# The last branch of a hybrid decoder layer: merge and weight splits in a fixed order on ScalarE, VectorE and POOL

## The chip, the cores and the metric

The kernel runs on one core of a Trainium2 chip. The metric is the time of one execution on the device in microseconds (us). Before the change it is 1801.29 us, the median of three runs (1801.08 to 1802.17). All times below that name a place in the program are counted from the start of the profiled execution's span.

## The reference

One decoder layer on 1024 tokens of width 1024, all in float32. Three branches (an RWKV-7 recurrence, a stick-breaking attention and a cross-attention into 256 memory tokens) each give 512 columns per token. They are projected, gated, summed and projected again; a convolutional feed-forward network follows.

```python
h = rms_norm(x, norm1_g[l])
proj = h @ w_in[l]
p_rwkv, p_sb, q_mem, gate_logits = jnp.split(proj, cut, axis=-1)
y_a, v_first = rwkv7_branch(p_rwkv, ...)
y_b = stick_breaking_branch(p_sb, ...)
y_m = memory_branch(q_mem, mem, ...)
ys = jnp.stack([y_a, y_b, y_m], axis=2)
branch_out = jnp.einsum('btnc,ncd->btnd', ys, w_branch[l])
gates = jax.nn.sigmoid(gate_logits.reshape(b, t, N_BRANCH, D_MODEL))
merged = jnp.sum(gates * branch_out, axis=2)
x = x + merged @ w_out[l]
x = x + conv_ffn(x, norm2_g[l], w_up[l], conv_w[l], conv_b[l], w_down[l])
```

The place in question is `branch_out` and `merged` for the first branch (`y_a`, done last, because its recurrence ends last), and the start of `merged @ w_out`.

## The kernel before

**Products in three parts.** Each float32 operand is split into a high part, rounded to the format that TensorE multiplies fast, and a low part, the remainder. A product is the sum of three: high by high, high by low, low by high (`mm3`). So every weight tile of 128 x 1024 that comes from HBM is split before use (`split_raw`): ScalarE copies it into the high part (line 80), POOL subtracts that from the raw tile and writes the low part (line 81). Raw tiles arrive through `load_w` on SP's queue, in two buffers named `wr`. A new load into such a buffer can only be issued after POOL's half of the split that read it.

**The last branch** (`branch_last`). `y` holds the first branch's output, split, in four tiles. The result is made in eight blocks d = 0 to 7 of 128 output columns each, over all 1024 tokens in two halves. For a block, TensorE runs 24 matmuls (four tiles of `y`, three parts, two halves) into one pair of PSUM banks. Four banks named `mm` make two pairs, which the blocks use in turn. A branch weight `w_br` serves two blocks, so there are four of them. Then:

- VectorE multiplies each half in PSUM by the gate tile `g`, loaded from `gsd` (line 1286). This frees the bank.
- VectorE adds the partial sum `o` of the other two branches, loaded from `mrd` (line 1287).
- ScalarE copies the result into the high part of the merged tile `mg` (line 1293: one piece of 512 tokens, two of 256), VectorE subtracts and writes the low part (line 1294).

**The output projection** (`out_proj`) follows. It takes the merged tiles as stationary operand and eight tiles of `w_out`, split by `load_wo`, as moving one. The first four of these splits are called for inside `branch_last`, at d = 2 to 5, the other four in `out_proj`. Its first step computes two token tiles at once, in both pairs of banks, with 12 matmuls for each of the eight weight tiles.

**What sets the order.** Most of the program leaves the order of instructions on an engine to a scheduler, which works with estimated times. `keep_in_program_order` fixes an instruction's place among the others that are marked so, on its engine. In `branch_last` nothing is marked. Buffers limit the loads: there are seven `at` tiles, four of which hold `y`, so three are left for the gates, and a fourth gate waits until block 0's last subtraction; three `w4` tiles hold the partial sums. SP issues its DMAs in one order, and a DMA whose buffer is not free holds back those behind it.

In front of the last branch stands the last gate block: TensorE makes the logits, ScalarE empties the banks (line 820), VectorE multiplies (line 821), ScalarE applies the sigmoid (line 824) and stores (line 826). Block 1 of the last branch uses the banks that line 820 empties. Line 1192 is VectorE's half of the split of `y`.

Of the kernel before, what the change touches and what calls it, by code (L numbers as in the profile page):

```python
# [11 lines left out]
F32 = mybir.dt.float32  # L12
F32R = mybir.dt.float32r
BF16 = mybir.dt.bfloat16
AF = mybir.ActivationFunctionType
ALU = mybir.AluOpType
# [33 lines left out]
class Trunk:  # L50
# [25 lines left out]
        self.nc.sync.dma_start(raw, src)  # L76
        return raw

    def split_raw(self, raw, hi, lo):
        self.nc.scalar.activation(hi, raw, AF.Copy)  # L80
        self.nc.gpsimd.tensor_tensor(lo, raw, hi.bitcast(F32), ALU.subtract)  # L81
        return hi, lo

    def split_w(self, src):
        raw = self.load_w(src)
        hi = self.pool_wt.tile([128, 1024], F32R, name=self.nm("wh"), tag="wh", bufs=2)
        lo = self.pool_wt.tile([128, 1024], F32R, name=self.nm("wl"), tag="wl", bufs=2)
        return self.split_raw(raw, hi, lo)

    def mm3(self, outs, w, x, first, last):  # L90
        for pi, (a, b) in enumerate(((0, 0), (0, 1), (1, 0))):
# [1159 lines left out]
            items.append(self.branch_item(b, d, st, first))  # L1251
        return load, hooks, items

    def load_wo(self, k):
        slots = ["qk"] * 8 + ["at"] * 6 + ["it", "sp"]
        hl = [self.pool_l.tile([128, 1024], F32R, name="wo_sp", tag="sp", bufs=1) if s == "sp" else self.t4(s, F32R) for s in slots[2 * k : 2 * k + 2]]
        self.wo.append(self.split_raw(self.load_w(self.I["w_out"][k]), *hl))

    def branch_last(self):
        nc = self.nc  # L1260
        self.wo = []
        y = self.split_y(self.yT, True)
        mg = lambda name, shape: self.pool_l.tile(shape, F32R, name=name, tag="l4")
        self.mg0 = [[mg(f"mg0_{i}_{k}", [128, 2, 512]) for k in range(4)] for i in range(2)]
        self.mg1 = [[[mg(f"mg1_{i}_{t}_{k}", [128, 4, 256]) for k in range(2)] for t in range(2)] for i in range(2)]
        for d in range(8):
            if d % 2 == 0:
                w = self.split_w(self.I["w_br"][0, d // 2])
            g, o = self.t4("at"), self.t4()
            nc.sync.dma_start(g, self.gsd[0, d])  # L1270
            nc.sync.dma_start(o, self.mrd[d])
            pp = [self.ps("mm"), self.ps("mm")]
            if d == 0:
                for i, (a, b) in enumerate(((0, 0), (1, 0), (0, 1))):
                    for k in range(4):
                        for h in range(2):
                            self.mmul(pp[h], w[a][:, k * 256 : k * 256 + 128], y[k][b][:, h * 512 : (h + 1) * 512],
                                      start=(i == 0 and k == 0), stop=(i == 2 and k == 3))
            else:
                for k in range(4):  # L1280
                    self.branch_mm(d, w, y, pp, k)
            if d in (2, 3, 4, 5):
                self.load_wo(d - 2)
            for h in range(2):
                hs = slice(h * 512, (h + 1) * 512)
                nc.vector.tensor_tensor(g[:, hs], pp[h], g[:, hs], ALU.mult)
                nc.vector.tensor_tensor(g[:, hs], g[:, hs], o[:, hs], ALU.add)  # L1287
                if h == 0:
                    parts = [[self.mg0[i][d // 2][:, d % 2] for i in range(2)] + [slice(0, 512)]]
                else:  # L1290
                    parts = [[self.mg1[i][t][d // 4][:, d % 4] for i in range(2)] + [slice(512 + 256 * t, 768 + 256 * t)] for t in range(2)]
                for hi, lo, ts in parts:
                    nc.scalar.activation(hi, g[:, ts], AF.Copy)
                    nc.vector.tensor_tensor(lo, g[:, ts], hi.bitcast(F32), ALU.subtract)  # L1294

    def out_proj(self):
        nc = self.nc
# [745 lines left out]
```

## Time and profile before

| | |
|---|---|
| median of three runs | 1801.29 us |
| the profiled execution | 1802.26 us |
| its span, first to last instruction | 1800.5 us |
| mean granted TensorE clock | 0.999 |

The profile names engines as follows: PE is TensorE, PEld its weight loads, DVE VectorE, ACT ScalarE, POOL GpSimd; SPq is the queue of SyncE, which issues most DMAs. A row of the timeline gives start, length, engine, line, operation, the tile written and the tiles read, the count of instructions merged in it, and in brackets the engine's idle time ahead of the first of them and what ended it. A row of the waits names who waited for whom, with the total in us, the times and the longest. A row of the windows gives the stretch, its length, the busy time of the engine asked for with its count of instructions, the granted clock, the mean busy share of the DMA engines and what they moved in GB/s.

### The profile page before, as it was taken

What the parts mean: (1) busy time and instruction counts of PE and PEld (TensorE: products, weight loads), DVE (VectorE), ACT (ScalarE), POOL (GpSimd) and SP (SyncE); (2) the same over time, 40 slices, a digit from 0 to 9 for tenths busy, and PEclk for the clock granted to TensorE, in tenths of its full rate; (3) what the DMA queues carried; (4) which work ended last, traced back from release to release, by engine and by line L of the source; (5) the groups of instructions that cost most, each with busy time, mean ns of one, the idle gap of its engine ahead of it and who ended that gap; (6) DMA issues with size and microseconds to landing.
All of it is one profiled execution on the core that took longest, in us unless ns stands there. A gap on an engine that the chain in (4) does not pass through costs nothing.

```text
span 1800.5 us, 27327 instructions
## 1 busy us (share of the span) xinstructions
PE 1778.4 (99%) x10479; PEld 1443.3 (80%) x10479; DVE 1183.7 (66%) x1626; ACT 864.3 (48%) x1556; POOL 791.5 (44%) x448
## 2 busy tenths in 40 slices
PE   9999999999999999999999999999999999999999
PEld 6777778888888888777777878877888888888887
DVE  5667774898987625244443882587776777785496
ACT  6444344556566636544444334554544444454343
POOL 3223353322322462122423541587767767545454
PEclk9999999999999999999999999999999999999999
DMA  5155564211112352567654462322322323486475
GB/s 209 59 164 176 194 210 158 74 42 45 53 57 77 118 138 69 185 238 274 230 189 176 164 222 94 117 88 99 117 96 88 122 95 111 135 303 229 147 237 207
DMA packets 122773, 261.29 MB, mean 145 GB/s; under 512 B 28682, under 2 KB 43658, under 8 KB 122515
## 3 DMA queue, kind: packets, MB, share of 16 engines
q1 hardware_dynamic: 85026, 193.83, 32.5%
q10 hardware_dynamic: 33840, 53.10, 8.0%
q0 software_dynamic: 3776, 12.62, 2.3%
q8 instruction: 82, 1.34, 0.3%
q14 instruction: 49, 0.39, 0.1%
HBM read 178.99 MB, written 80.48 MB: 144 GB/s over the span
## 4 chain that ended last, share of the span: by engine, by line
PE 69%; DVE 6%; ACT 2%; issue 2%; POOL 2%; DMA 1%; SPq 0%; DVEq 0%; POOLq 0%; ACTq 0%
PE mm L115 57%; PE g L115 10%; PE g L105 3%; DMA wr<-in_w_out_dram 1%; DVE at L926 1%; DVE mg L1294 1%; DVE it L545 1%; DMA A<-yd 1%; DVE at L1287 0%; POOL wl L81 0%; POOL wl L1465 0%; DVE inst L547 0%; DVE gall L1550 0%; ACT at L1143 0%; DVE w L821 0%
## 5 line engine op out<-in xcount | busy, mean ns | idle before, releaser
L81 POOL TENSOR_TENSOR wl<-wr,wh 128x1024 fp32r<-128x1024 f32 (+2 forms) x78 | 195.9, 2513 | 501.9 <-ACT wh L80 492.2
L115 PE MATMUL mm<-xhi,wh 128*128 128x512 f32 x784 | 259.9, 412 | 0.5 <-DVE w L322 0.4
L115 PE MATMUL mm<-xlo,wh 128*128 128x512 f32 x784 | 243.7, 392 | 0.2 <-DVE xlo L199 0.2
L115 PE MATMUL mm<-xhi,wl 128*128 128x512 f32 x784 | 242.5, 391 | 0.0
L115 PEld LDWEIGHTS mm<-xlo,wh 128*128 128x128 f32 x784 | 147.2, 188 | 33.7 <-DVE xlo L199 0.9
L115 PEld LDWEIGHTS mm<-xhi,wl 128*128 128x128 f32 x784 | 146.9, 188 | 33.0 <-POOL wl L81 0.7
L115 PEld LDWEIGHTS mm<-xhi,wh 128*128 128x128 f32 x784 | 136.7, 189 | 28.9 <-issue 6.1
L80 ACT ACTIVATE wh<-wr 128x1024 fp32r<-128x1024 f32 (+2 forms) x78 | 81.8, 1048 | 146.2 <-PE mm L115 94.1
L115 PE MATMUL mm<-dw,da 128*128 128x512 f32 x528 | 120.3, 389 | 0.0
L115 PE MATMUL mm<-BT,l 128*128 128x512 f32 x504 | 117.9, 389 | 1.4 <-POOL l L1465 1.4
L115 PEld LDWEIGHTS mm<-dw,da 128*128 128x128 f32 x528 | 99.1, 188 | 20.6
L1754 POOL TENSOR_TENSOR dw<-draw,dw 128x512 fp32r<-128x512 f32 x55 | 82.0, 1498 | 76.4 <-ACT dw L1752 69.0
L115 PEld LDWEIGHTS mm<-BT,l 128*128 128x128 f32 x504 | 94.5, 188 | 21.4 <-POOL l L1465 1.8
L926 DVE TENSOR_TENSOR_SCAN at<-at,nrt 128x128 f32<-128x128 f32 (+3 forms) x64 | 94.2, 1478 | 25.5 <-ACT at L920 25.3
L115 PE MATMUL mm<-BT,wh 128*128 128x512 f32 x352 | 108.6, 389 | 0.9 <-DVE BT L1375 0.9
L115 PE MATMUL mm<-B,wh 128*128 128x512 f32 x352 | 108.4, 389 | 0.0
L1753 DVE TENSOR_TENSOR da<-draw,da 128x512 fp32r<-128x512 f32 x77 | 63.4, 830 | 50.9 <-ACT da L1751 50.7
L115 PE MATMUL g<-dw,da 128*128 128x512 f32 x396 | 90.2, 389 | 0.0
L1465 POOL TENSOR_TENSOR l<-it,l 128x1024 fp32r<-128x1024 f32 x21 | 50.8, 2419 | 88.9 <-ACT l L1462 88.8
L821 DVE TENSOR_TENSOR w<-w,nrt 128x1024 f32<-128x1024 f32 x24 | 49.8, 2076 | 58.5 <-ACT w L820 47.5
L115 PEld LDWEIGHTS g<-dw,da 128*128 128x128 f32 x396 | 74.3, 188 | 15.4
L1751 ACT ACTIVATE da<-draw 128x512 fp32r<-128x512 f32 x77 | 48.1, 628 | 79.2 <-PE mm L115 31.8
(335 smaller groups left out, 3990.0 us busy)
## 6 DMA issues: line engine op xcount, KB each, us to landing
wr<-in_w_in_dram SPq DMA_DIRECT2D x48, 512.0 KB, 3.6
draw<-actd SPq DMA_DIRECT2D x77, 256.0 KB, 3.2
draw<-in_w_down_dram SPq DMA_DIRECT2D x55, 256.0 KB, 4.5
at<-scr SPq DMA_DIRECT2D x24, 512.0 KB, 5.9
wr<-in_w_up_dram SPq DMA_DIRECT2D x22, 512.0 KB, 3.5
actd<-gall ACTq DMA_DIRECT2D x44, 256.0 KB, 3.2
rw<-in_w_up_dram SPq DMA_DIRECT2D x20, 512.0 KB, 3.6
gsd<-w ACTq DMA_DIRECT2D x18, 512.0 KB, 2.8
```

Of the source, the lines that this page charges most:

```text
L80: self.nc.scalar.activation(hi, raw, AF.Copy)
L81: self.nc.gpsimd.tensor_tensor(lo, raw, hi.bitcast(F32), ALU.subtract)
L105: self.pinned(self.nc.tensor.transpose(out, in_, self.ident[:n, :n]))
L115: self.pinned(self.nc.tensor.matmul(*a, **k))
L545: self.pinned(nc.vector.tensor_tensor(tv, X[:, 0:s, s : s + 1].to_broadcast([128, s, n]), X[:, s : s + 1, s + 1 : 64].to_broadcast([128, s ...
L821: nc.vector.tensor_tensor(g, g, self.nrb, ALU.mult)
L926: self.pinned(nc.vector.tensor_tensor_scan(sn[:, :W][:, ::-1], sn[:, :W][:, ::-1], self.nrt[:, 1152 - W :][:, ::-1], 1.0, ALU.mult, ALU.max))
L1294: nc.vector.tensor_tensor(lo, g[:, ts], hi.bitcast(F32), ALU.subtract)
L1465: ins = nc.gpsimd.tensor_tensor(lo, src, hi.bitcast(F32), ALU.subtract)
L1751: self.pinned(nc.scalar.activation(A[:, 0], a, AF.Copy))
L1753: self.pinned(nc.vector.tensor_tensor(A[:, 1], a, A[:, 0].bitcast(F32), ALU.subtract))
L1754: nc.gpsimd.tensor_tensor(Wt[:, 1], w, Wt[:, 0].bitcast(F32), ALU.subtract)
```

## The change

`split_raw`, `split_w` and `load_wo` get a parameter through which the caller can fix their instructions' order. `branch_last` uses it. The first two branch weights and the first output weight are called for ahead of the block loop; inside the loop each of blocks 0 to 4 calls for one more weight after its own work: output weight 1 after block 0, branch weight 2 after block 1, output weight 2 after block 2, branch weight 3 after block 3, output weight 3 after block 4. The multiplies, adds, copies and subtractions are marked as fixed, in the order two multiplies, two adds with the copies, three subtractions.

```diff
-    def split_raw(self, raw, hi, lo):
-        self.nc.scalar.activation(hi, raw, AF.Copy)
-        self.nc.gpsimd.tensor_tensor(lo, raw, hi.bitcast(F32), ALU.subtract)
+    def split_raw(self, raw, hi, lo, fix=lambda ins: ins):
+        fix(self.nc.scalar.activation(hi, raw, AF.Copy))
+        fix(self.nc.gpsimd.tensor_tensor(lo, raw, hi.bitcast(F32), ALU.subtract))
         return hi, lo
...
     def branch_last(self):
...
+        fix = self.tc.keep_in_program_order
+        ws = [self.split_w(self.I["w_br"][0, j]) for j in range(2)]
+        self.load_wo(0)
         for d in range(8):
-            if d % 2 == 0:
-                w = self.split_w(self.I["w_br"][0, d // 2])
+            w = ws[d // 2]
             g, o = self.t4("at"), self.t4()
...
-            if d in (2, 3, 4, 5):
-                self.load_wo(d - 2)
+            halves = []
             for h in range(2):
                 hs = slice(h * 512, (h + 1) * 512)
-                nc.vector.tensor_tensor(g[:, hs], pp[h], g[:, hs], ALU.mult)
-                nc.vector.tensor_tensor(g[:, hs], g[:, hs], o[:, hs], ALU.add)
+                fix(nc.vector.tensor_tensor(g[:, hs], pp[h], g[:, hs], ALU.mult))
+            for h in range(2):
+                hs = slice(h * 512, (h + 1) * 512)
+                fix(nc.vector.tensor_tensor(g[:, hs], g[:, hs], o[:, hs], ALU.add))
...
                 for hi, lo, ts in parts:
-                    nc.scalar.activation(hi, g[:, ts], AF.Copy)
-                    nc.vector.tensor_tensor(lo, g[:, ts], hi.bitcast(F32), ALU.subtract)
+                    fix(nc.scalar.activation(hi, g[:, ts], AF.Copy))
+                    halves.append((lo, g[:, ts], hi.bitcast(F32)))
+            for lo, x, hi in halves:
+                fix(nc.vector.tensor_tensor(lo, x, hi, ALU.subtract))
+            if d in (1, 3):
+                ws.append(self.split_w(self.I["w_br"][0, d // 2 + 2], fix))
+            elif d in (0, 2, 4):
+                self.load_wo({0: 1, 2: 2, 4: 3}[d], fix)
```

The built programs hold the same instructions, and TensorE and VectorE run them in the same order as before. On the three other engines the order differs, in the last branch alone.

ScalarE, from the split of the first output weight (`qk<-wr`) into block 1; `wh` are high parts of branch weights, L820 empties the gate block's banks, `mg` are the merged tiles. Before:

```order
L80 ACTIVATE qk_9574<-wr_9576 128x1024
L820 ACTIVATE w_1457_9410<-mm_9360 128x512
L820 ACTIVATE w_1457_9410<-mm_9361 128x512
L80 ACTIVATE wh_9540<-wr_9538 128x1024
L824 ACTIVATE w_1457_9410<-w_1457_9410 128x1024
L826 DMA gsd<-w_1457_9410 128x1024
L80 ACTIVATE qk_9620<-wr_9622 128x1024
L1293 ACTIVATE mg_0_0_9436<-at_9458 128x512
L1293 ACTIVATE mg_0_0_0_9444<-at_9458 128x256
L1293 ACTIVATE mg_0_1_0_9446<-at_9458 128x256
L80 ACTIVATE wh_9638<-wr_9636 128x1024
L1293 ACTIVATE mg_0_0_9436<-at_9498 128x512
```

ScalarE at the same place now (L1296 is the former L1293):

```order
L80 ACTIVATE qk_9464<-wr_9466 128x1024
L80 ACTIVATE wh_9460<-wr_9458 128x1024
L820 ACTIVATE w_1457_9410<-mm_9360 128x512
L820 ACTIVATE w_1457_9410<-mm_9361 128x512
L824 ACTIVATE w_1457_9410<-w_1457_9410 128x1024
L826 DMA gsd<-w_1457_9410 128x1024
L1296 ACTIVATE mg_0_0_9436<-at_9470 128x512
L1296 ACTIVATE mg_0_0_0_9444<-at_9470 128x256
L1296 ACTIVATE mg_0_1_0_9446<-at_9470 128x256
L80 ACTIVATE qk_9510<-wr_9512 128x1024
L1296 ACTIVATE mg_0_0_9436<-at_9516 128x512
```

The second output weight's split stood ahead of block 0's copies and stands behind them now; the second branch weight's split stood behind L820 and stands ahead of it.

POOL, the low parts of the splits of the last branch; `qk` and `at` belong to output weights, `wl` to branch weights. Before:

```order
L81 TENSOR_TENSOR qk_9575<-wr_9576,qk_9574 128x1024
L81 TENSOR_TENSOR wl_9541<-wr_9538,wh_9540 128x1024
L81 TENSOR_TENSOR qk_9621<-wr_9622,qk_9620 128x1024
L81 TENSOR_TENSOR wl_9639<-wr_9636,wh_9638 128x1024
L81 TENSOR_TENSOR qk_9673<-wr_9674,qk_9672 128x1024
L81 TENSOR_TENSOR qk_9719<-wr_9720,qk_9718 128x1024
L81 TENSOR_TENSOR wl_9737<-wr_9734,wh_9736 128x1024
L81 TENSOR_TENSOR at_9821<-wr_9822,at_9820 128x1024
```

POOL at the same place now:

```order
L81 TENSOR_TENSOR qk_9465<-wr_9466,qk_9464 128x1024
L81 TENSOR_TENSOR wl_9461<-wr_9458,wh_9460 128x1024
L81 TENSOR_TENSOR qk_9511<-wr_9512,qk_9510 128x1024
L81 TENSOR_TENSOR wl_9559<-wr_9556,wh_9558 128x1024
L81 TENSOR_TENSOR qk_9603<-wr_9604,qk_9602 128x1024
L81 TENSOR_TENSOR wl_9651<-wr_9648,wh_9650 128x1024
L81 TENSOR_TENSOR qk_9695<-wr_9696,qk_9694 128x1024
L81 TENSOR_TENSOR at_9821<-wr_9822,at_9820 128x1024
```

Output and branch weights alternate now; before, the third and fourth output weight followed each other ahead of the last branch weight.

SP's DMAs, from the second branch weight on; `at<-gsd` are gates, `w<-mrd` partial sums. Before:

```order
L76 DMA wr_9538<-in_w_br_dram 128x1024
L1270 DMA at_9458<-gsd 128x1024
L1270 DMA at_9498<-gsd 128x1024
L1270 DMA at_9544<-gsd 128x1024
L76 DMA wr_9576<-in_w_out_dram 128x1024
L1271 DMA w_1470_9459<-mrd 128x1024
L1271 DMA w_1474_9499<-mrd 128x1024
L76 DMA wr_9622<-in_w_out_dram 128x1024
L76 DMA wr_9636<-in_w_br_dram 128x1024
```

SP at the same place now (L1272 and L1273 are the former L1270 and L1271):

```order
L76 DMA wr_9458<-in_w_br_dram 128x1024
L1272 DMA at_9470<-gsd 128x1024
L76 DMA wr_9466<-in_w_out_dram 128x1024
L1272 DMA at_9516<-gsd 128x1024
L1272 DMA at_9562<-gsd 128x1024
L76 DMA wr_9512<-in_w_out_dram 128x1024
L1273 DMA w_1476_9471<-mrd 128x1024
L1273 DMA w_1483_9517<-mrd 128x1024
L76 DMA wr_9556<-in_w_br_dram 128x1024
```

The first output weight moved ahead of the gates of blocks 1 and 2, and the second one ahead of the partial sums of blocks 0 and 1.

More of the change, by code (lines that the diff above doesn't have):

```diff
@@ L77, in load_w, with split_w @@
         return raw
-    def split_raw(self, raw, hi, lo):
-        self.nc.scalar.activation(hi, raw, AF.Copy)
-        self.nc.gpsimd.tensor_tensor(lo, raw, hi.bitcast(F32), ALU.subtract)
+    def split_raw(self, raw, hi, lo, fix=lambda ins: ins):
+        fix(self.nc.scalar.activation(hi, raw, AF.Copy))
+        fix(self.nc.gpsimd.tensor_tensor(lo, raw, hi.bitcast(F32), ALU.subtract))
         return hi, lo
-    def split_w(self, src):
+    def split_w(self, src, fix=lambda ins: ins):
         raw = self.load_w(src)
@@ L87, in split_w @@
         lo = self.pool_wt.tile([128, 1024], F32R, name=self.nm("wl"), tag="wl", bufs=2)
-        return self.split_raw(raw, hi, lo)
+        return self.split_raw(raw, hi, lo, fix)
     def mm3(self, outs, w, x, first, last):
@@ L1252, in branch, with load_wo @@
         return load, hooks, items
-    def load_wo(self, k):
+    def load_wo(self, k, fix=lambda ins: ins):
         slots = ["qk"] * 8 + ["at"] * 6 + ["it", "sp"]
         hl = [self.pool_l.tile([128, 1024], F32R, name="wo_sp", tag="sp", bufs=1) if s == "sp" else self.t4(s, F32R) for s in slots[2 * k : 2 * k + 2]]
-        self.wo.append(self.split_raw(self.load_w(self.I["w_out"][k]), *hl))
+        self.wo.append(self.split_raw(self.load_w(self.I["w_out"][k]), *hl, fix))
     def branch_last(self):
```

## The prediction

> **What bounds the kernel now.** I read the busy times first, then the waits of one window, then the order of time.
>
> ```profile
> span 1800.5 us, 27327 instructions
> ...
> PE 1778.4 (99%) x10479; PEld 1443.3 (80%) x10479; DVE 1183.7 (66%) x1626; ACT 864.3 (48%) x1556; POOL 791.5 (44%) x448
> ```
>
> TensorE is busy for 1778.4 of 1800.5 us: 22 us of idle time in the whole program. A change that takes no matmul away can therefore gain only where PE pauses or runs slowly. Everything the diff touches lies between the last gate block and the output projection, about 1018 to 1078 us. The waits of that window:
>
> ```profile
> PEld mm L115 <- DVE at L1286: 5.3, 7, 1.8
> ...
> PE mm L115 <- DVE at L1286: 2.4, 3, 1.3
> ```
>
> PE waits there for one thing: VectorE's multiply L1286, which empties the two PSUM banks of a block. Banks come in two pairs, so block d+2 starts only when block d has been multiplied. The PE rows show what the waits cost:
>
> ```profile
> 1018.36 1.98 PE L115 MATMUL mm<-at,wh 128*128 128x512 f32 x8
> ...
> 1034.23 0.61 PE L115 MATMUL mm<-at,wl 128*128 128x512 f32 x2
> 1036.18 1.09 PE L115 MATMUL mm<-at,wh 128*128 128x512 f32 x2 [1.33 <-DVE at L1286]
> 1037.11 0.63 PE L115 MATMUL mm<-A,wh 128*128 128x512 f32 x2
> ...
> 1048.12 1.09 PE L115 MATMUL mm<-at,wh 128*128 128x512 f32 x2 [0.40 <-DVE at L1286]
> ...
> 1065.38 1.52 PE L115 MATMUL mm<-qk,mg 128*128 128x512 f32 x6
> 1067.59 10.19 PE L115 MATMUL mm<-qk,mg 128*128 128x512 f32 x42 [0.68 <-DVE at L1286]
> 1077.61 8.32 PE L115 MATMUL mm<-at,mg 128*128 128x512 f32 x36
> 1085.77 0.61 PE L115 MATMUL mm<-it,mg 128*128 128x512 f32 x2
> ```
>
> Unhindered, 36 matmuls take 1085.77 - 1077.61 = 8.16 us, 0.2267 each. From 1018.36 to 1077.61 stand 8 x 24 of the last branch and 48 of the output projection: 240 x 0.2267 = 54.41 us, against 59.25 elapsed. **PE loses 4.84 us here.** A gap costs more than its idle time: the pair after the first one took 1037.11 - 1036.18 = 0.93 instead of 0.45, so 0.48 on top. 4.84 us is also the most that the change can gain, since 1018.36 is set by the gate block's matmuls, which stay.
>
> Why is the multiply late? VectorE's time from one block's first multiply to the next one's (length, then its busy time):
>
> ```profile
> 1024.36:1035.45 11.09, 8.77 (x9) 1.00 0.75 256
> 1035.45:1039.30 3.85, 3.75 (x8) 1.00 0.73 254
> 1039.30:1047.39 8.09, 6.67 (x9) 1.00 0.75 292
> 1047.39:1053.27 5.88, 5.88 (x9) 1.00 0.80 258
> 1053.27:1057.12 3.85, 3.75 (x9) 1.00 0.89 306
> 1057.12:1060.97 3.85, 3.75 (x8) 1.00 0.96 343
> 1060.97:1066.85 5.88, 5.88 (x8) 1.00 0.34 122
> 1066.85:1074.46 7.61, 7.61 (x8) 1.00 0.37 115
> ```
>
> A block needs 3.85 us; PE gives it 24 x 0.2267 = 5.44. But blocks 0, 2 and 7 took 11.09, 8.09 and 7.61. The same instruction is short or long by what POOL does:
>
> ```profile
> L1286 DVE TENSOR_TENSOR at<-mm,at x16: 673/678/683, 1024.4 to 1067.5; 128x512 f32<-128x512 f32 x16
> ...
> L1287 DVE TENSOR_TENSOR at<-at,w x16: 674/680/2885, 1025.6 to 1070.3; 128x512 f32<-128x512 f32 x16
> ...
> L81 POOL TENSOR_TENSOR qk<-wr,qk x4: 2395/2618/2840, 1021.0 to 1044.0; 128x1024 fp32r<-128x1024 f32 x4
> ```
>
> The multiply, with one operand in PSUM, never exceeds 0.683. The add L1287 (and L1294), with both in SBUF, reaches 2.885: it stands still while POOL runs a split's second half (2.40 undisturbed). Blocks 1, 4 and 5 met no split, 3 and 6 one, 0, 2 and 7 two.
>
> **The change part by part.** No instruction is added or removed. PE's and VectorE's orders stay the same; the diff's regrouped VectorE loop writes down what the scheduler already chose, cost 0 by that. What moves is ScalarE's, POOL's and SP's order.
>
> *One split per block.* The new ScalarE order puts one split behind each block's copies L1293, so POOL's half starts at a fixed distance:
>
> ```profile
> 1055.17 1.33 ACT L1293 ACTIVATE mg<-at 128x512 fp32r<-128x512 f32 x3 [2.34 <-DVE at L1287]
> ...
> 1061.09 1.06 ACT L80 ACTIVATE at<-wr 128x1024 fp32r<-128x1024 f32 x1 [0.73 <-DVE mg L1294]
> ```
> ```profile
> 1062.23 2.88 POOL L81 TENSOR_TENSOR at<-wr,at 128x1024 fp32r<-128x1024 f32 x1 [10.71 <-ACT at L80]
> ```
>
> Copies end at 1055.17 + 1.33 = 1056.50, 0.62 before the next block's first multiply (1057.12). POOL begins 1.14 after a split's ScalarE half starts (1062.23 - 1061.09), so about 0.5 into the next block, and ends 2.40 later at 2.9. The first 1.2 us of a block are the two multiplies, which POOL does not touch; the adds then wait 2.9 - 1.2 = 1.7. **An estimate of 3.85 + 1.7 = 5.55 us per block with a split** against PE's 5.44: nearly even. The measured rows with one split give 5.88, because there the split began later and hit an add. I take 5.5, nearly PE's pace, so that VectorE falls behind by 0.1 a block at most, and keep 5.88 as the other end. The weights still come early: a branch split ends about 3 us into a VectorE block, and PE begins the block that uses it 5.4 us into the same one.
>
> *Block 0 and SP's queue.* What can spoil this is the start. On SP the first output weight (wo0) now goes ahead of two gate loads, and the second (wo1), which waits for POOL to finish with wo0's buffer, ahead of the partial sum of block 0 (o0, read by the first add):
>
> ```profile
> 1008.48 3.13 SPq L1270 DMA_DIRECT2D at<-gsd  x3
> 1013.08 0.33 SPq L76 DMA_DIRECT2D wr<-in_w_out_dram  x1
> 1016.41 6.20 SPq L1271 DMA_DIRECT2D w<-mrd  x2
> 1023.38 0.33 SPq L76 DMA_DIRECT2D wr<-in_w_out_dram  x1
> ```
> ```profile
> 1019.81 1.06 ACT L80 ACTIVATE qk<-wr 128x1024 fp32r<-128x1024 f32 x1 [7.92 <-DMA wr<-in_w_out_dram]
> 1020.77 1.07 ACT L820 ACTIVATE w<-mm 128x512 f32<-128x512 f32 x2
> ```
> ```profile
> 1020.96 2.40 POOL L81 TENSOR_TENSOR qk<-wr,qk 128x1024 fp32r<-128x1024 f32 x1 [3.66 <-ACT qk L80]
> ```
> ```profile
> 1025.56 2.30 DVE L1287 TENSOR_TENSOR at<-at,w 128x512 f32<-128x512 f32 x2
> ```
>
> Times to landing: output and branch weights, then partial sums, then gates:
>
> ```profile
> DMA to landing us min/median/max: 3.5/4.1/6.6
> ```
> ```profile
> DMA to landing us min/median/max: 3.7/4.5/5.4
> ```
> ```profile
> DMA to landing us min/median/max: 3.2/5.2/7.3
> ```
>
> wo0 is issued at 1013.08 as before. It landed after 6.7 us behind three gates; behind one I take the median 4.1, so 1017.2, with 1019.8 as the other end. ScalarE's half and the lead to POOL (1.14) and POOL's 2.40 give wo1's issue at 1020.8 to 1023.4 and o0's 0.4 later, 1021.2 to 1023.8, where it used to go out at 1016.41. With 4.5 (5.4 at the late end) it lands at 1025.7 to 1029.2; I take 1026.5, a little after the early end, because wo1 is ahead of it. The add began at 1025.56 before, so the cover that the early load had is gone: it may wait 1 to 3.6 us. But block 0 no longer has two splits on it, and ScalarE's copies no longer stand behind wo1's split. Two adds (1.28) and the rest (1.35) end 2.6 after landing, about 1029.1 (late: 1031.8), when PE has just finished block 1 (1018.36 + 48 x 0.2267 = 1029.24). **VectorE is level with PE after block 0**, or 2.6 late.
>
> The Trainium skill, "DMA: Bandwidth & Descriptors", section "Anatomy of one DMA", fits 2.0 us plus bytes over 436 GB/s for POOL's path, which would be 3.2 us for 512 KB: o0 would then land before 1025.6, and the gain would be the full 4.8. The rows here show 3.7 at best and 4.5 in the middle, so the measurement decides.
>
> *Other waits.* The two gates moved behind wo0 go out near 1013.5; at 7.3 they land by 1021, and block 1 needs its gate at 1029. ScalarE's eviction L820 now stands behind a second split: its end, 1020.77 + 1.07 = 1021.84, becomes 1022.9 if wo0 lands as late as before, while PE wants that bank for block 1 at 1018.36 + 5.44 = 1023.80. Cover 0.9 us; beyond it PE pays one for one. The fourth output split now stands behind the last branch split; PE needs it only in the projection, three blocks later.
>
> *Sum.* At the boundary the projection has six matmuls (1.36 us) before it needs block 7's banks, and the first multiply takes 0.68, so a lag of up to 0.6 is free. The level start plus 0.1 for each of blocks 1 to 6 gives about 0.6, the edge of what is free; I charge one short pause with its 0.48, some 0.5. Gain 4.84 - 0.5 = **4.3 us**. The profiled execution took 1802.26 (span 1800.5 and 1.76 around it), 0.97 above the median of the runs, 1801.29. So 1798.0 for it and **1797.0** by the median. With o0 at its late end the lag is 2.6, the loss 2.6 - 0.6 + 0.48 = 2.5, the gain 2.3.
>
> **The rivals.** *VectorE becomes the bound.* If each block with a split takes the measured 5.88, it falls behind by 0.44 six times before block 7's multiply, 2.6 us, plus the start. Loss 2.6 - 0.6 + 0.48 = 2.5 and some 0.5 for the start: gain 1.8, time 1799.5. For it: both one-split rows. Against: in them the split began inside an add, not 0.5 us into the block.
>
> *Slower: the partial sum is starved.* o0 shares the DMA engines with wo1, o1, the gate store and the next branch weight. At the 256 GB/s of block 0's row these 2.6 MB take 10.2 us; if o0 finishes with the last of them, it lands at 1023.8 + 10.2 = 1034.0, VectorE is 1034.0 + 2.6 - 1029.24 = 7.4 us late after block 0, and the loss is 7.4 - 0.6 + 0.48 = 7.3, 2.4 worse than now: 1803.7. It decides from a landing near 1031.6, where the loss passes 4.84. Against: no partial sum took over 5.4. The Trainium skill (same page, "Issuing engines are not separate DMA queues") says that DMAs of all issuers run on the same 16 engines and interleave; this gives the rival a mechanism. No row here shows a partial sum held that long.
>
> *The splits do not matter.* If the late multiplies came from elsewhere, or the time saved is lost again in the projection, nothing changes: 1801.3. Against: the add's 0.68 against 2.885.
>
> **How the numbers follow.** A measurement of this kernel can tell about 0.2%, 3.6 us, from no change; the forecast of 4.3 lies just beyond. Chances: forecast 0.66, of which 0.08 falls between gains of 2.3 and 3.6 with a late o0; VectorE bound 0.18; starved 0.07; no effect 0.09. So faster 0.58, same 0.35, slower 0.07. Range: 4.84 gained is 1796.45, less 0.25 for the scatter of the runs, 1796.2; upward it takes in VectorE as the bound (1799.5) and, on top, an o0 a further 1.1 us late: 1800.6.
>
> **What would show it.** Right: PE rows from 1018 to about 1073 with no gap over 0.3 us and no slow pair; the first add near 1027; every block with a split about 5.5 us in VectorE's windows; POOL never with two splits in a row before block 7. VectorE as the bound: multiplies later by 0.4 with each block, and a gap of some 3 us only at the projection. Starved: the add of block 0 waits for the partial sum's DMA past 1031. Wrong altogether if PE's 240 matmuls take 54.5 us and the total still stays.

## The result, and the profile after

| | before | changed |
|---|---|---|
| median of the runs compared, us | 1801.37 (1798.21 to 1803.46, 21 runs) | 1799.11 (1797.58 to 1800.48, 21 runs) |
| profiled execution, us | 1802.26 (span 1800.5) | 1798.70 (span 1796.9) |

The ratio of the two is 0.9986 with a 95% interval of 0.9980 to 0.9991: a small gain of 2.3 us, where 4.3 was forecast, inside the forecast range and less than the 0.2% that the prediction counted as telling. A second comparison gave 1799.52 against 1802.34 (0.9988, 0.9979 to 0.9996).

The head of the profile page of the changed kernel, with the busy times:

```profile
span 1796.9 us, 27324 instructions
...
PE 1776.8 (99%) x10479; PEld 1443.2 (80%) x10479; DVE 1180.5 (66%) x1626; ACT 864.6 (48%) x1556; POOL 790.5 (44%) x448
```

The waits of TensorE between 1018 and 1074 us (engine, line, what it waited for: total, times, longest):

```profile
PEld mm L115 <- DVE at L1287: 0.4, 1, 0.4
```

Before, the same stretch had seven such waits with 5.3 us on the weight loads and three with 2.4 us on the matmuls. What is left is the boundary to the output projection (start, length, group; the first row is the last branch's first matmul):

```profile
1017.99 1.98 PE L115 MATMUL mm<-at,wh 128*128 128x512 f32 x8
...
1061.05 0.62 PE L115 MATMUL mm<-at,wl 128*128 128x512 f32 x2
1061.51 11.34 PE L115 MATMUL mm<-qk,mg 128*128 128x512 f32 x48
1072.68 3.56 PE L115 MATMUL mm<-at,mg 128*128 128x512 f32 x15
```

The last branch started at 1017.99 here, so the 240 matmuls took 1072.68 - 1017.99 = 54.69 us against 54.41 unhindered. **The loss fell from 4.84 to 0.28 us.** The projection began at 1061.51 instead of 1065.38.

POOL's rows show one split per block, and VectorE's rows what that makes of a block:

```profile
1017.26 3.21 POOL L81 TENSOR_TENSOR qk<-wr,qk 128x1024 fp32r<-128x1024 f32 x1 [0.35 <-ACT qk L80]
1020.45 3.37 POOL L81 TENSOR_TENSOR wl<-wr,wh 128x1024 fp32r<-128x1024 f32 x1
1029.09 2.40 POOL L81 TENSOR_TENSOR qk<-wr,qk 128x1024 fp32r<-128x1024 f32 x1 [5.27 <-PE mm L115]
1034.43 2.40 POOL L81 TENSOR_TENSOR wl<-wr,wh 128x1024 fp32r<-128x1024 f32 x1 [2.94 <-ACT wh L80]
1039.77 2.40 POOL L81 TENSOR_TENSOR qk<-wr,qk 128x1024 fp32r<-128x1024 f32 x1 [2.94 <-ACT qk L80]
...
1057.72 2.46 POOL L81 TENSOR_TENSOR at<-wr,at 128x1024 fp32r<-128x1024 f32 x1 [4.88 <-PE mm L115]
```
```profile
1018.14 3.42 DVE L1192 TENSOR_TENSOR A<-qk,at 128x1024 fp32r<-128x1024 f32 x1
1021.49 3.42 DVE L821 TENSOR_TENSOR w<-w,nrt 128x1024 f32<-128x1024 f32 x1
1024.82 1.28 DVE L1287 TENSOR_TENSOR at<-mm,at 128x512 f32<-128x512 f32 x2
1026.02 1.28 DVE L1290 TENSOR_TENSOR at<-at,w 128x512 f32<-128x512 f32 x2
...
1028.84 1.29 DVE L1287 TENSOR_TENSOR at<-mm,at 128x512 f32<-128x512 f32 x2
...
1034.28 1.29 DVE L1287 TENSOR_TENSOR at<-mm,at 128x512 f32<-128x512 f32 x2 [0.18 <-PE mm L115]
1035.48 2.50 DVE L1290 TENSOR_TENSOR at<-at,w 128x512 f32<-128x512 f32 x2
...
1056.04 1.29 DVE L1287 TENSOR_TENSOR at<-mm,at 128x512 f32<-128x512 f32 x2 [0.59 <-PE mm L115]
...
1061.92 1.28 DVE L1287 TENSOR_TENSOR at<-mm,at 128x512 f32<-128x512 f32 x2
```

A multiply (L1287, formerly L1286) now waits for PE, by 0.18 us in block 2 and 0.59 in block 6: VectorE keeps pace and even gains on TensorE. The splits repeat every 5.34 us, TensorE needs 5.44 a block, so each split meets its block 0.1 us earlier and the pairs of adds (L1290) shrink, from 2.60 us in block 1 and 2.50 in block 2 to 2.19 in block 5.

So 4.6 us went away where the change works. The profiled executions differ by 3.6, the medians by 2.3 to 2.8. Of the 3.6, 0.4 came ahead of this place (1018.36 became 1017.99) and 1.3 were lost behind it: from 1077.61 to the end of the span it was 722.9 us, and from 1072.68 it is 724.2. The experiments ask where the rest is. One visible place is the clock, in the up phase (PEclk is the granted clock, 1.00 full):

```profile
core 0: us, PE busy (x) PEld busy (x) DVE busy (x) ACT busy (x) POOL busy (x), PEclk, DMA share, GB/s
1213.75:1217.16 3.41, 1.33 (x6) 0.75 (x4) 3.38 (x5) 0.82 (x1) 3.33 (x3) 1.00 0.63 244
1217.16:1220.57 3.41, 3.23 (x8) 2.59 (x9) 2.46 (x5) 2.42 (x4) 3.41 (x3) 0.50 0.19 68
```

After a window with a pause of 2.26 us, TensorE ran 3.41 us at half clock, which costs up to 1.7 us (an estimate: half of 3.41). The kernel before has the same pause, and no half clock after it in its profile; it has such a stretch at 624 us, behind another pause.

### The profile page after: what moved, and what is told of

The parts are those of the page before. It is cut to its first block, busy times and chain, and to the rows that moved or that the text cites. A ratio compares the mean times of both kernels' runs of the same rounds, so it can differ in the third digit from the quotient of the medians.

```text
span 1796.9 us, 27324 instructions
## 1 busy us (share of the span) xinstructions
PE 1776.8 (99%) x10479; PEld 1443.2 (80%) x10479; DVE 1180.5 (66%) x1626; ACT 864.6 (48%) x1556; POOL 790.5 (44%) x448
## 4 chain that ended last, share of the span: by engine, by line
PE 72%; DVE 5%; ACT 2%; POOL 2%; issue 1%; DMA 1%; DVEq 0%; POOLq 0%; ACTq 0%; SPq 0%
PE mm L115 60%; PE g L115 10%; PE g L105 3%; DVE at L926 1%; DVE it L545 1%; DMA A<-yd 1%; DVE inst L547 1%; POOL wl L1474 0%; DVE gall L1559 0%; ACT at L1143 0%; DVE w L821 0%; DVE qk L866 0%; DVE qk L865 0%; POOL wl L81 0%; DVE w L854 0%
## 5 line engine op out<-in xcount | busy, mean ns | idle before, releaser
L821 DVE TENSOR_TENSOR w<-w,nrt 128x1024 f32<-128x1024 f32 x24 | 50.7, 2114 | 56.3 <-ACT w L820 45.4
```

The source lines that it names most:

```text
L821: nc.vector.tensor_tensor(g, g, self.nrb, ALU.mult)
```

## The experiments

Losses are those of the same 240 matmuls throughout. Each set of four runs has its own theories, so the letters in the second and third set are not those of the first.

**1. The same two kernels again: how steady is each?** before_a and before_b are the kernel before, after_a is the changed one, with no edit.

> The kernel before, unchanged, timed against itself and profiled again. Two theories for why the change gave 2.3 us in the median and not the 4.6 that its trace shows between 1018 and 1073 us. Theory A (the pause of the profiled execution was a long one): how long the last branch holds TensorE up differs from execution to execution of the kernel before, by when the first output weight lands (6.7 us after its issue in the profile). Then this profile shows another loss than 4.84 us over the 240 matmuls from the branch's first one, anywhere from 1 to 5, and single times scatter by some 5 us (1798 to 1803.5) as in the runs shown. Theory B (half-clock stretches): each profile shows one stretch of 3.41 us at half clock, worth some 1.7 us; the changed kernel has one more of them in about half its executions, and the kernel before has not. Then the loss is again 4.8 us within 0.3, and the mean clock of these runs is 0.999 nearly always.

> The kernel before once more, for a third profile of the same program. Theory A: a loss over the 240 matmuls that differs from the two other profiles by over 0.5 us in at least one of them, together with a different landing time of the first output weight. Theory B: 4.8 us within 0.3.

> The changed kernel, unchanged, timed and profiled again. Theory A: the 240 matmuls take 54.7 us within 0.2 (a loss of 0.3), whatever else varies; the runs lie in two groups some 1.8 us apart with clocks 0.999 and 0.998, as likely as for the kernel before; the ratio is 0.9986 within its interval (0.998 to 0.9991). Theory B: the same loss, but clock 0.998 in half of the runs against nearly none for the kernel before.

Measured: before_a 1802.67 us (ratio to the kernel before 0.9999, 0.9990 to 1.0007), after_a 1799.52; the single run of before_b 1800.70. Losses: 3.34 (1018.31 to 1076.06) and 4.85 (1017.06 to 1076.32) before, 0.28 again after the change (1018.48 to 1073.17). Half-clock stretches: one in before_a (at 625), none in before_b, two in after_a (at 624 and 1218). So the old order's loss varies from run to run, the new one's does not (0.28 in the profiles of after_sums and after_fill below, too), and the stretches vary in both.

**2. Is it POOL's time in a block?** In pool_twice the POOL half of each split of blocks 0 to 4 is done twice.

```diff
+        if self.twice:
+            fix(self.nc.gpsimd.tensor_tensor(lo, raw, hi.bitcast(F32), ALU.subtract))
```

> The changed kernel with POOL's half of each split of blocks 0 to 4 done twice (same values, written again). If VectorE's adds stand still while POOL runs (theory), a block grows from 5.35 to about 5.35 + 2.4 = 7.75 us in five blocks, VectorE falls 2.3 behind PE in each, 11.5 in all, and with free slack 0.6 and restarts PE loses 11 to 13 us: time about 1811. Rival (POOL's work does not hold VectorE, the long adds are a coincidence of the record): PE loses 0.3 as before, time 1799.

Measured: a loss of 12.02 us, time 1807.78 us.

```profile
1040.60 0.73 PE L118 MATMUL mm<-at,wl 128*128 128x512 f32 x2 [1.12 <-POOL wl L84]
1055.60 0.81 PE L118 MATMUL mm<-at,wl 128*128 128x512 f32 x2 [3.48 <-POOL wl L84]
1071.42 11.83 PE L118 MATMUL mm<-qk,mg 128*128 128x512 f32 x42 [2.61 <-DVE at L1291]
```

VectorE's blocks took 7.5 us (first multiplies at 1034.78, 1042.29 and 1049.84), near the 7.75 expected: a block with 2.4 us more of POOL is no longer inside PE's 5.44, and one split per block is about what fits. The loss of 12.02 lies in the range that was worked out (11 to 13), but in part by luck. The pauses make 7.21 us of it, and only the last one is VectorE's; in the two others TensorE waited for a branch weight whose doubled split ended late. Two half-clock stretches within the 240 matmuls, at 1056 and 1073 us, cost up to 3.4 more. The time is 3 us below the 1811 expected; this profile has no stretch anywhere else.

**3. Can a pair of splits be covered?** In pair_b2 the third and fourth output weight are both split behind block 2, none behind block 4.

```diff
-            elif d in (0, 2, 4):
-                self.load_wo({0: 1, 2: 2, 4: 3}[d], fix)
+            elif d in (0, 2):
+                self.load_wo({0: 1, 2: 2}[d], fix)
+                if d == 2:
+                    self.load_wo(3, fix)
```

> The changed kernel, but the third and the fourth output weight are both split behind block 2, and none behind block 4: two splits follow each other once. If a block of slack covers them (VectorE needs 5.3 us for a block with one split, 7.6 with two, TensorE gives 5.44 and is two banks ahead), the 240 matmuls from the last branch's first one lose at most 0.3 to 0.8 us, against 0.28 in the changed kernel. If two splits in a row are what makes a pause wherever they stand, as in the kernel before, a pause of 1 to 2 us comes at block 5, with a slow pair of 0.48 behind it: a loss of 1.7 to 2.7.

Measured: loss 0.96 us, time 1798.66. POOL's rows:

```profile
1040.38 2.40 POOL L81 TENSOR_TENSOR qk<-wr,qk 128x1024 fp32r<-128x1024 f32 x1 [2.94 <-ACT qk L80]
1043.82 2.40 POOL L81 TENSOR_TENSOR qk<-wr,qk 128x1024 fp32r<-128x1024 f32 x1 [1.04 <-ACT qk L80]
```

There was no pause at block 5; the pair only made the boundary later. Neither number was hit (0.3 to 0.8, or 1.7 to 2.7), but the reading with slack is the nearer: with VectorE level with PE, one pair in the middle costs 0.7 us (one run).

**4. The places or the fixed order?** old_fixed keeps the fixed order and calls the splits at the old places (first diff); moved_free (second) has the new places, and its ScalarE, VectorE and POOL are ordered by the scheduler.

```diff
+            if d % 2 == 0:
+                w = self.split_w(self.I["w_br"][0, d // 2], fix)
...
+            if d in (2, 3, 4, 5):
+                self.load_wo(d - 2, fix)
```
```diff
-        fix = self.tc.keep_in_program_order
+        fix = lambda ins: ins
```

> The changed kernel's fixed order, but the splits called at the old places: the second to fourth branch weight at the start of the block that uses them, the output weights ahead of blocks 2 to 5. If the places are what gains: a branch weight's split now follows the copies of the block before and ends about 3.5 us behind them, while TensorE wants it at once, so it waits 5 to 7 us at blocks 2, 4 and 6, and the 240 matmuls lose 15 to 20 us: about 1814 to 1819. If the fixed order by itself is what gains: a loss under 1 us, as in the changed kernel.

> The changed kernel's code with the splits at their new places, but ScalarE, VectorE and POOL ordered by the scheduler: ScalarE then has the second output weight's split ahead of block 0's copies, and POOL runs the first three output weights nearly in a row. If the new places alone gain (weights called earlier): a loss under 0.5 us over the 240 matmuls. If one split per block is what counts: two splits meet block 0 or 1, and the loss is 1.5 to 3.4, as in the kernel before.

Measured: old_fixed loses 23.42 us (1822.69), moved_free 6.72 (1806.53). Both are slower than the kernel before; each is a single run. First rows of old_fixed, with the window behind its first pause (columns as above: PE's busy time first, PEclk 0.50), then of moved_free:

```profile
1033.90 1.22 PE L115 MATMUL mm<-at,wh 128*128 128x512 f32 x2 [4.06 <-ACT wh L80]
1036.35 1.22 PE L115 MATMUL mm<-at,wl 128*128 128x512 f32 x2 [0.38 <-POOL wl L81]
```
```profile
1033.66:1040.48 6.82, 6.21 (x14) 4.43 (x15) 0.00 (x0) 1.13 (x2) 4.70 (x2) 0.50 0.69 226
```
```profile
1048.08 2.41 POOL L81 TENSOR_TENSOR qk<-wr,qk 128x1024 fp32r<-128x1024 f32 x1 [9.27 <-ACT qk L80]
1050.45 2.80 POOL L81 TENSOR_TENSOR wl<-wr,wh 128x1024 fp32r<-128x1024 f32 x1
```
```profile
1054.61 1.30 PE L115 MATMUL mm<-at,wh 128*128 128x512 f32 x2 [2.97 <-DVE at L1287]
```

In old_fixed PE waits for each branch weight, as expected; in moved_free a pair of splits, late in the phase, leaves a pause of 2.97. Both cost more than forecast (15 to 20, and 1.5 to 3.4): each long pause, three in old_fixed and one in moved_free, was followed by 6.8 us at half clock, 3.4 us more each time. Without that, by an estimate, moved_free would lose about 3.3, as forecast, and old_fixed about 13, less than forecast, because its pauses took 4.06 and not 5 to 7. So in these two variants neither part of the change gains alone.

**5. Does the distance of the pause at 1215 us decide the stretches?** delay puts 20 more matmuls, whose result nothing reads, ahead of the output projection, so that later stages stand where they stood before the change.

```diff
+        idle = self.ps("g")
+        for _ in range(20):
+            self.mmul(idle, self.mg0[0][0][:, 0, :128], wo[0][0][:, :512], start=True, stop=True)
```

> The changed kernel, with 20 more matmuls of 128x512 ahead of the output projection, into a bank that nothing reads; the output stays the reference's. They take 20 x 0.2267 = 4.53 us, about the time that the change took away, so that all that follows stands where it stood in the kernel before. Theory A with a fixed grid (the place of the later pause on the 3.41 us grid decides how often it draws a stretch): the stretch at 1217 becomes as rare as before, and the delay costs 4.53 less 0.8 to 1.6 = 2.9 to 3.7 us. Theory B: the full 4.5 us, or 4.3 if the extra matmuls also cover the last pause of 0.3 us at 1063.

Measured: 1803.82 us, 4.7 above the first table's changed kernel and 4.3 above after_a. The full cost came back, so a fixed shift of the grid does not explain the missing gain. (The extra matmuls covered the last pause, too: the other 240 matmuls lost nothing.)

**6. What if the pause at 1215 us is shortened?** after_sums and before_sums move two of four sums on VectorE behind the adds that empty the bank.

```diff
-                    act_sums(pairs[n - 1][1], True)
+                    else:
+                        act_sums(pairs[n - 1][1], True)
...
+                if n == 2:
+                    act_sums(pairs[n - 1][1], True)
```

> The changed kernel, with two of the four sums of the gates (3.44 us of VectorE) moved behind the two adds that empty a bank, in the up phase near 1210 us. They delayed these adds, and TensorE idled 2.26 us at 1215 for it. Theory A (half-clock stretches eat the rest of the gain): the pause goes, and with it the stretch of 3.41 us at half clock that followed it in both profiles of the changed kernel, 1.6 us more. So 2.3 + 1.3 to 1.6 = 3.6 to 3.9 us less than the changed kernel, 1795.5, no stretch at 1217, and 4.0 us less than the kernel before with the same edit. Theory B (stretches are chance and take the same from both kernels): 2.3 to 3.3 less, about 1796.5, and 2.8 less than the kernel before with the same edit, as without it. Third: VectorE is late at the next bank instead, the pause moves, and nothing is gained.

> The kernel before, with the same edit of the up phase. Theory A: of its profiles none had a stretch at 1217, so it gains the pause of 2.3 us and less than 0.8 besides: about 1799.4, and stays 3.9 to 4.0 above the changed kernel with the edit. Theory B: it gains as much as the changed kernel does, 2.3 to 3.3, about 1799.3, and stays 2.8 above it.

Measured: 1799.16 us and 1803.44 us. The third case came, in both: the pause is still there, a little later and longer, and now for POOL (after_sums):

```profile
1221.78 0.50 PE L115 MATMUL mm<-B,wl 128*128 128x512 f32 x1 [2.49 <-POOL wl L1474]
```

VectorE had hidden POOL there. The edit says nothing of the stretches, since both kernels had one behind the new pause. Their difference is 4.3 us; the loss of before_sums was 3.08.

**7. What if the two pauses are filled?** after_fill and before_fill put 9 matmuls, whose result is overwritten, into each of the pauses at 621 and 1215 us.

```diff
+            if h == 0:
+                for _ in range(9):
+                    self.mmul(pk, mhi[0][:, :128], mhi[0][:, :512], start=True, stop=True)
...
+                if n == 2:
+                    for _ in range(9):
+                        self.mmul(Dk, self.B["11"][0][0][:, 0, :128], self.B["11"][0][0][:, 0], start=True, stop=True)
```

> The changed kernel, with 9 matmuls of 128x512 whose result is overwritten put into each of TensorE's two pauses of 2.27 us, at 621 and at 1215 us; the output stays the reference's. They take 9 x 0.2267 = 2.04 us each, less than the pause. Theory A (a pause of 2.3 us draws a stretch of 3.41 us at half clock, which costs 1.7): no stretch is left but the one at the very end, and the kernel gains what the mean of its runs has lost to them, 1.6 x 1.7 = 2.7 us: about 1796.5, and the runs lie within 1 us of each other. Theory B (the stretches have another cause): they stay, and the time stays at 1799.3, or grows if the matmuls delay others.

> The kernel before, with the same 18 matmuls in the same two pauses. Theory A: it loses its stretches too, 1.3 x 1.7 = 2.2 us, so about 1799.9. Then only the part around the last branch tells the two apart, and before_fill stays 3.4 to 4.1 us above after_fill (its loss over the 240 matmuls was 3.1 to 4.85 in four profiles, the changed kernel's 0.28), against 2.8 without the fill. Theory B: both stay as they were, and so does the 2.8.

Measured: after_fill 1797.11 us (1796.31 to 1798.00, 7 runs; ratio to the kernel before 0.9973, 0.9962 to 0.9984), before_fill 1799.39 (1797.68 to 1800.82, 11 runs; 0.9985, 0.9976 to 0.9994). In after_fill:

```profile
core 0: 1795.4 us, clock 1.000
```
```profile
1211.43 2.20 PE L115 MATMUL mm<-B 128*128 128x512 f32 x9
...
1216.59 3.00 PE L115 MATMUL mm<-B,l 128*128 128x512 f32 x12 [0.24 <-DVE u L1610]
```

All 7 runs of after_fill and 10 of the 11 of before_fill show a mean clock of 1.000. The stretches come from these two pauses, and **after_fill has the lowest median of all kernels here**, by 18 matmuls that compute nothing. (It was not timed beside the changed kernel, and the intervals of their ratios to the kernel before, 0.9962 to 0.9984 and 0.9980 to 0.9991, overlap a little.) But the other half of the theory fell: without stretches the two kernels stand 2.3 us apart, not 3.4 to 4.1; from the earlier 2.8 the scatter of the runs does not separate it. So most of the missing gain did not go into stretches; the loss of the old order must be smaller in most runs than in the first profile. One reason is seen in before_fill, first ScalarE's start of wo0's split, then POOL and PE; the landing times of the gates and of output weights in the old order (the last number, in us) are those of the kernel before, of before_fill and of before_sums:

```profile
1017.23 1.06 ACT L80 ACTIVATE qk<-wr 128x1024 fp32r<-128x1024 f32 x1 [5.40 <-DMA wr<-in_w_out_dram]
```
```profile
1018.39 2.43 POOL L81 TENSOR_TENSOR qk<-wr,qk 128x1024 fp32r<-128x1024 f32 x1 [1.14 <-ACT qk L80]
1020.78 3.37 POOL L81 TENSOR_TENSOR wl<-wr,wh 128x1024 fp32r<-128x1024 f32 x1
```
```profile
1046.30 1.09 PE L115 MATMUL mm<-at,wh 128*128 128x512 f32 x2 [0.40 <-DVE at L1290]
1065.78 10.18 PE L115 MATMUL mm<-qk,mg 128*128 128x512 f32 x42 [0.71 <-DVE at L1290]
```
```profile
at<-gsd SPq DMA_DIRECT2D x3, 512.0 KB, 6.4
wr<-in_w_out_dram SPq DMA_DIRECT2D x2, 512.0 KB, 6.6
```
```profile
at<-gsd SPq DMA_DIRECT2D x3, 512.0 KB, 3.7
wr<-in_w_out_dram SPq DMA_DIRECT2D x2, 512.0 KB, 4.1
```
```profile
at<-gsd SPq DMA_DIRECT2D x3, 512.0 KB, 3.3
wr<-in_w_out_dram SPq DMA_DIRECT2D x2, 512.0 KB, 3.5
```

With the same order on the queue, wo0 landed after 6.6 or 6.7 us in three executions (the first profile, before_a and before_b) and after 4.1 or 3.5 in two. Where it landed early, the first two splits were over before the adds of block 0 (POOL done at 1024.15 here, at 1026.7 in the first profile), the pause of 1.33 us at block 2 with its 0.48 was not there, and the loss was 3.14 and 3.08. The profiled run of before_fill took 1800.67, 1.3 above the median of its kernel, so the old order may well lose less than 3 us in other runs; no profile shows such a one.

## Why the prediction came out as it did

The range held the time and the sign was right, but the gain was 2.3 to 2.8 us for a forecast of 4.3. That the range held it is in part luck: it reached up to 1800.6 for a VectorE that is the bound and a late o0, the time is close to the 1799.5 of that rival, and the profile shows neither.

- **What bounds the kernel: right.** PE's pauses were VectorE's late multiplies, and these came from POOL's splits. moved_free (2.97 us) and the last pause of pool_twice (2.61) bring them back through this chain. The other pauses of pool_twice and all of old_fixed came another way, through a branch weight that was split too late. One row was misread: three splits touched block 0, not two (the end of that from 1023.33, and those from 1029.70 and 1032.25).
- **One split per block: right, and somewhat better.** 5.55 us a block was estimated, a little over PE's 5.44. The splits come every 5.34, start 0.25 us behind the multiply in block 1 and 0.15 in block 2 and not 0.5, and VectorE gains 0.1 a block where a lag of 0.1 was charged.
- **Block 0 and SP's queue: right in the outcome.** wo1 went out at 1020.51 and o0 at 1020.89 (forecast 1020.8 and 1021.2). The first add started at 1026.02, right behind its multiplies, and block 0 was done at 1028.84 (forecast 1029.1). The multiply itself started at 1024.82, 0.46 later than before: L1192 and L821 took 3.42 us each beside two splits.
- **The loss that stays: 0.28 for 0.5.**
- **The rivals.** VectorE did not become the bound: 5.88 occurs only in block 6, whose split begins 1.7 us into it. The partial sum was not starved. The splits do matter.
- **The step that failed** is the first number of the sum, "4.84". It was read from one profiled execution as what the old order costs, and the offset of 0.97 us between that execution and the median was subtracted from the total, as if it lay outside the pauses. The profiles of the old order lose 4.84, 3.34, 4.85, 3.08 and 3.14 us, 3.85 on average. The sentence "It landed after 6.7 us behind three gates" took for a property of the queue what is one of at least two outcomes of the same order. In two of the three low profiles wo0 landed early; in before_a it took 6.6 us, and the pause at block 2 was missing all the same. There wo1's split began 0.68 us earlier on POOL than in the first profile, as the two rows show (before_a, then the first profile). ScalarE's copy ahead of it started 4.60 us after the load's issue, against 5.18 there and 5.12 in before_b, which has the pause. So this landing varies, too; that it is the reason wasn't tried.

```profile
1029.02 2.40 POOL L81 TENSOR_TENSOR qk<-wr,qk 128x1024 fp32r<-128x1024 f32 x1 [2.41 <-ACT qk L80]
```
```profile
1029.70 2.40 POOL L81 TENSOR_TENSOR qk<-wr,qk 128x1024 fp32r<-128x1024 f32 x1 [2.99 <-ACT qk L80]
```

With 3.85 in place of 4.84 the sum gives 3.85 - 0.28 = 3.6. The three pairs of kernels that differ by this change alone differ in their medians by 2.3 to 2.8 (plain), 4.3 (sums) and 2.3 (filled). A mean over five profiles whose values lie 1.8 us apart is no sharper than that. A true loss of about 3 us fits the plain and the filled pair; the sums pair would need 4.6, and how the loss is spread over the runs stays open.

The prediction also has no term for the stretches, though its first profile holds one. Every profile with a mean clock of 1.000 has no stretch (the one at the very end of the span aside), those with 0.999 have one and those with 0.998 two. Counted so, the plain runs of the changed kernel draw 1.58 on average (33 runs, none with 1.000), and those of the kernel before 1.22 (81 runs, 13 with 1.000): at some 1.7 us each, an estimate of 0.6 us that the change loses there. In delay, whose later stages stand where they stood before the change, 2 of 12 runs have 1.000 again, but its time did not follow.

## What to carry to other kernels

A pause that rests on when a DMA lands can be there in one execution and gone in the next, so read it in several profiles before its length goes into a sum as the gain. When VectorE and POOL work from the same memory, spacing POOL's pieces by one per block of TensorE's work can be worth more than where any one of them stands; here it took both the early call and the fixed order. In a kernel that keeps TensorE 99% busy, a pause of 2 us may cost nearly twice its length, and cheap matmuls that compute nothing can be worth their place in it.

## What the runs showed of the hardware that was not expected

The half-clock stretches lie on a grid of 3.41 us whose position against the start of the span differs from run to run. Around the two pauses, at 621 and 1215 us, every window of the grid in which PE was busy for 1.33 us or less was followed by one at half clock, and none with 1.49 or more. The row with 1.33 stands with the result; that with 1.49 is from before_b (PE's busy time behind the length):

```profile
1216.95:1220.36 3.41, 1.49 (x7) 0.91 (x5) 3.38 (x5) 0.68 (x1) 3.25 (x4) 1.00 0.58 227
1220.36:1223.78 3.42, 3.09 (x14) 2.55 (x14) 2.46 (x5) 2.79 (x5) 3.42 (x2) 1.00 0.25 90
```

So the same pause of 2.27 us draws a stretch or not, by where the grid cuts it.

This bears on why the changed kernel draws more. In after_a 174 windows lie between the starts of its two stretches (623.95 and 1217.87), so a window is 3.413 us. There the second pause ends 174.0 windows after the first (623.86 and 1217.83): the grid cuts both alike, and both drew a stretch. In the first profile of the changed kernel, where the first pause drew none, it is 173.6, and the second one drew. In the kernel before it is 174.8 to 175.3, the grid cuts the second pause elsewhere, and it drew none in three profiles. That this is why none of the 33 runs was without a stretch is not shown.

The Trainium skill, "TensorE: Matmul & The Clock Gate", section "Part 1: The HAM clock gate (the "warmup" mystery)", describes a free-running window of 3413 ns and a clock that is half or full; the traces agree with both (windows of 3.413 us, a clock of 0.50 or 1.00). It puts the half clock after an idle window; here a window that was busy for 39% of its time was enough.

The stretching of VectorE and POOL by each other goes both ways: L1192 took 3.42 us beside a split, against 1.21 with POOL idle, and the splits beside L1192 and L821 took 3.21 and 3.37 us instead of 2.40. The multiply, with one operand in PSUM, took at most 0.692 us in every profile. The Trainium skill, "SBUF — State Buffer", section "Who interferes with whom", says that a VectorE operation with two inputs in SBUF and one of GpSimd that reads SBUF exclude each other, and that one with a single such input does not take part; the rows agree.
